# Seven-product pairs in a SwiGLU gate and up projection: four k-pairs of eight in place of three, with half of their weight sums added by DMA

## The chip, the cores and the metric

The kernel runs on one core of a Trainium2 chip. The metric is the time of one execution on the device in microseconds; lower is better. Three runs of the kernel before gave 2144.05 us in the median (2143.3 to 2145.18). The numbers are float32 throughout.

## The reference, cut to what matters

One decoder layer on 256 tokens of width 2048: a half feed-forward block, a mixing stage with three branches, and a second half feed-forward block of the same form. The change lies in the two feed-forward blocks:

```python
def swiglu_half_ffn(x, norm_g, w_gate_up, w_down):
    h = rmsnorm(x, norm_g)
    gate, up = jnp.split(h @ w_gate_up, 2, axis=-1)
    return 0.5 * ((jax.nn.silu(gate) * up) @ w_down)
```

`w_gate_up` is 2048 x 11264, its first 5632 columns for the gate and the others for up. `w_down` is 5632 x 2048.

## The kernel before, in words

**Two rounds for each product.** TensorE multiplies in `float32r`, a rounded float32. To keep float32 accuracy, each operand is cut in two: `cut` (L235) has ScalarE write the rounded value of a weight tile (`wh`), and VectorE write the rest, tile minus rounded tile (`wl`). The activations are cut in the same way when they are transposed. `add_product` (L240) then issues three matmuls of 128 x 128 by 128 x 512: high by high, low by high, high by low.

**Groups of the gate and up weights.** A feed-forward block (`ffn`, L412) handles the 5632 columns in eleven chunks of 512. Chunk 0 goes through `mm_group` (L320), the plain way. Each of the chunks 1 to 10 is one call of `pair_group` (L247, called at L467), so there are ten such groups in each block and twenty in the kernel. A group makes four 128 x 512 results in PSUM: two halves of the tokens (t) by gate and up (n). It goes through the 2048 rows of the weights in eight k-pairs of 2 x 128 rows. For each pair two DMAs of 512 KB on SP's queue (L268) bring the gate and the up part, 1 MB together, into a `raw` buffer. There are three `raw` buffers (L266), shared with `mm_group`.

**Plain pairs and seven-product pairs.** A plain pair costs 2 x 2 x 2 products of three matmuls, 24 matmuls. Its weights are cut in two calls on 1024 columns (L275). A k-pair can also be seen as a 2 x 2 by 2 x 2 product of blocks and done with seven products in place of eight (Winograd's form of Strassen's method), 21 matmuls. Then the activations are combined beforehand into a `form` page (`form_page`, L214), one for each such pair, and sums of the weight blocks are needed:

- L286: cut of the first two blocks `s0`, `s1` (`plain`)
- L288: `ta` = two sums, `s3+s1` and `s3+s2`, in one VectorE operation on 128 x 1024; L290: its cut (`hah`, `hal`)
- L292: cut of `s2` (`plain2`)
- L293, L294: `tb` = two more sums, `ta0+s2` and then that plus `s0`, each one VectorE operation on 128 x 512; L296: its cut (`hbh`, `hbl`)

The seven products read, in order, `plain` twice, `ha` twice, `plain2` once and `hb` twice (L299 to L307). After the last seven-product pair, L312 to L316 combine four extra PSUM banks (`p1`, `p5`, `p6`, `p7`) into terms that are added to the four results at the end. All eight banks come from one pool of eight; the transposes of the hidden activations take banks from it as well.

**Order.** The tuple `MIXED` (L24) lists the k-pairs in the order in which they are taken; the pairs with a number below the count of `form` pages are seven-product pairs. With three pages `MIXED` gives: plain 3, seven 0, plain 4, seven 1, plain 5, seven 2, plain 6, plain 7. Other steps (turning the hidden activations of the chunk before, and storing them) wait in a queue of side steps. `tick` runs one of them after each half of a plain pair that stands behind the last seven-product pair (L280), so four in a group. `drain` (L477) runs what is left before the down projection. The program is laid out by a planner that simulates the time of the program and sets, engine by engine, a fixed order from it; on the chip each engine works through its own list in order and waits at semaphores.

**Pools.** `wh` and `wl` have five buffers each of 1024 columns (L229). Pages of 4 KB a partition (30, L64) hold the activations, forms, `ta`, `tb`, `hah`, `hal`, `hbh` and `hbl`.

Of the kernel before, what the change touches and what calls it, by code (L numbers as in the profile page):

```python
# [9 lines left out]
F32 = mybir.dt.float32  # L10
# [10 lines left out]
KD = D // P  # L21
FF = 5632
NFC = FF // 512
MIXED = (3, 0, 4, 1, 5, 2, 6, 7)  # L24
KF = FF // P
EPS = 1e-6
# [6 lines left out]
def hybrid_layer(  # L33
# [210 lines left out]
                ps, sides[part], wt[i][:, col : col + 512], start=start and q == 0, stop=stop and q == 2  # L244
            )

    def pair_group(w, c0, c1, lhs, forms, order):  # L247

        seven = [u for u in order if u < len(forms)]
        acc = {}
        sums = {}
        terms = []
        kinds = [(0, 0), (1, 0), (0, 1), (1, 1)]

        def into(key, last):
            if key not in acc:
                acc[key] = bank("mm")  # L260
                return acc[key], True, last
            return acc[key], False, last

        for i, u in enumerate(order):
            end = i == len(order) - 1
            raw = wp.tile([P, 2, 2, 512], F32, tag="raw", name="raw")  # L266
            for n, cc in enumerate((c0, c1)):
                nc.sync.dma_start(  # L268
                    out=raw[:, n, :, :],
                    in_=w[2 * u * P : (2 * u + 2) * P, cc : cc + 512].rearrange("(k p) c -> p k c", p=P),  # L270
                )
            if u not in seven:
                for n in range(2):
                    wt = parts(1024)
                    cut(wt, raw[:, n, :, :].rearrange("p k c -> p (k c)"))  # L275
                    for t in range(T):
                        for kk in range(2):
                            ps, start, stop = into((t, n), end and kk == 1)
                            add_product(ps, [lhs(2 * u + kk, q, t) for q in range(2)], wt, kk * 512, start, stop)
                    if i > order.index(seven[-1]) if seven else True:  # L280
                        tick()
                continue
            last = u == seven[-1]
            s = raw.rearrange("p n k c -> p (n k) c")
            plain = parts(1024)
            cut(plain, s[:, 0:2, :].rearrange("p s c -> p (s c)"))  # L286
            ta, tb = page([2, 512], F32, "ta"), page([2, 512], F32, "tb")
            nc.vector.tensor_tensor(ta, s[:, 3:4, :].to_broadcast([P, 2, 512]), s[:, 1:3, :], ALU.add)  # L288
            ha = (page([1024], F32R, "hah"), page([1024], F32R, "hal"))
            cut(ha, ta.rearrange("p s c -> p (s c)"))  # L290
            plain2 = parts(512)
            cut(plain2, s[:, 2, :])  # L292
            nc.vector.tensor_tensor(tb[:, 0, :], ta[:, 0, :], s[:, 2, :], ALU.add)  # L293
            nc.vector.tensor_tensor(tb[:, 1, :], tb[:, 0, :], s[:, 0, :], ALU.add)  # L294
            hb = (page([1024], F32R, "hbh"), page([1024], F32R, "hbl"))
            cut(hb, tb.rearrange("p s c -> p (s c)"))  # L296
            fm = lambda m: [forms[u][:, q, m, :] for q in range(2)]
            xq = lambda kk, t: [lhs(2 * u + kk, q, t) for q in range(2)]
            for key, sides, wt, col in (  # L299
                ("p1", xq(1, 0), plain, 512),  # L300
                ((0, 0), xq(0, 0), plain, 0),
                ("p5", fm(0), ha, 0),
                ("p7", fm(2), ha, 512),
                ((0, 1), fm(3), plain2, 0),
                ("p6", fm(1), hb, 0),
                ((1, 0), xq(0, 1), hb, 512),
            ):  # L307
                ps, start, stop = into(key, last if isinstance(key, str) else end)
                add_product(ps, sides, wt, col, start, stop)
            if last:  # L310
                a, u3, u4, v = (temp([512], n) for n in ("ua", "u3", "u4", "uv"))
                nc.scalar.activation(a, acc["p1"], AF.Copy)  # L312
                nc.vector.tensor_tensor(u3, acc["p6"], a, ALU.add)
                nc.vector.tensor_tensor(u4, acc["p5"], u3, ALU.subtract)
                nc.vector.tensor_tensor(u3, acc["p7"], u3, ALU.add)
                nc.vector.tensor_tensor(v, acc["p5"], u3, ALU.subtract)  # L316
                terms = {(0, 0): a, (1, 0): u3, (0, 1): u4, (1, 1): v}
        return acc, terms
# [93 lines left out]
    def ffn(lx, forms, rs, wgu, wd, stream, cb, before=None):  # L412
        hid, flat = [], {}
        hdram = dp.tile([NFC - 1, P, 4 * S], F32, tag="hd", name="hd", bufs=2)
        rh = st.tile([P, T], F32, tag="rh", name="rh")

        def put(c, hd):

            dst = []

            def turn(jj):
                if jj == 0:
                    dst.append(page([4, S], F32, "hf"))
                ps = aux([2, S], "hid")
                for j in range(2):
                    for t in range(T):
                        k = 2 * jj + j
                        nc.tensor.transpose(ps[:, j, t * P : (t + 1) * P], hd[t][:, k * P : (k + 1) * P], ident)  # L428
                nc.scalar.activation(dst[0][:, 2 * jj : 2 * jj + 2, :], ps, AF.Copy)
                if jj == 1:  # L430
                    nc.sync.dma_start(out=hdram[c], in_=dst[0].rearrange("p k s -> p (k s)"))

            return [lambda: turn(0), lambda: turn(1)]

        def get(c):
            if c < NFC - 1:
                flat[c] = page([4, S], F32, "hg")
                nc.sync.dma_start(out=flat[c].rearrange("p k s -> p (k s)"), in_=hdram[c])

        def use(c):  # L440
            if c < NFC - 1:
                f = flat.pop(c)
                for jj in range(2):
                    hid.append(page([2, 2, S], F32R, "hid"))
                    split(hid[-1], 0, 2, f[:, 2 * jj : 2 * jj + 2, :])

        def gated(c, gate, up):
            hd = []
            for t in range(T):
                s = gate[t]  # L450
                if c == 0:
                    s = temp([512], "sg")
                nc.scalar.activation(s, gate[t], AF.Silu, scale=rs[0][:, t : t + 1])
                h = temp([512], "hd") if c == 0 else up[t]
                nc.vector.scalar_tensor_tensor(h, up[t], rh[:, t : t + 1], s, ALU.mult, ALU.mult)
                hd.append(h)
            return hd

        pa = mm_group(wgu, 0, KD, lx, before=before)
        nc.vector.tensor_scalar(rh, rs[0], 0.5, None, ALU.mult)  # L460
        pb = mm_group(wgu, FF, KD, lx)
        hd = gated(0, [pa[t][0] for t in range(T)], [pb[t][0] for t in range(T)])
        side.extend(put(0, hd))
        for c in range(1, NFC):
            if c == NFC - 1:
                side.extend(put_last)
            acc, terms = pair_group(wgu, c * 512, FF + c * 512, lx, forms, MIXED)  # L467
            for n in range(2):
                for t in range(T):
                    d = terms[t, n]  # L470
                    nc.vector.tensor_tensor(d, acc[t, n], d, ALU.add)
            hd = gated(c, [terms[t, 0] for t in range(T)], [terms[t, 1] for t in range(T)])
            if c < NFC - 1:
                side.extend(put(c, hd))
            if c == NFC - 2:
                put_last = [lambda: get(0), lambda: get(1)]
        drain()  # L477
        use(0)
        last = to_lhs(hid, lambda t: hd[t], None, "hid")

        def need(n, k0):
            if k0 == KF - 8:
                stream.load(n)
            if n > 0:
                return
            c = k0 // 4
            if c + 2 < NFC - 1:
                get(c + 2)
            if c + 1 < NFC - 1:
                use(c + 1)  # L490
            elif c + 1 == NFC - 1:
                for f in last:
                    f()

        lh = lhs_of(hid)
        for c in range(4):
            ps = mm_group(wd, c * 512, KF, lh, need=lambda k0, c=c: need(c, k0))
            cb(c, [[ps[t][0]] for t in range(T)])
# [29 lines left out]
        side.append(lambda c=c: prepare(c, 1))  # L528
    side.append(lambda: row_sums(range(4)) or rs0.append(row_rstd(ss0, "x0")))
    forms0 = []  # L530
    side.extend(form_steps(forms0, tiles0))
    side.append(small_loads)
    side.extend(pause * 3 + [small_cols])
    s0 = Stream([xv[:, :, c * 512 : (c + 1) * 512] for c in range(4)])
# [378 lines left out]
    side.extend(pause * 2)  # L913
    for n in range(2):
        cb(2 + n, sums(po, terms, n))
    side.extend(form_steps(forms2, x2))


    def store(c, ps):
# [37 lines left out]
```

## Time and profile before

| What | Value |
| --- | --- |
| Median of three runs | 2144.05 us (2143.3 to 2145.18) |
| The profiled execution's own time | 2142.92 us |
| Its span, first to last instruction | 2141.2 us, granted clock 1.00 |
| TensorE matmul busy | 2132.6 us |
| VectorE busy | 1572.0 us |
| ScalarE busy | 1135.9 us |
| GpSimd busy | 3.5 us |
| Read from HBM | 426.16 MB |

All three runs and the profiled execution lie within 2.3 us of each other. Busy time is the union of an engine's instructions. Matmuls are pipelined, and their ends are modelled, so the share of TensorE is no measure of its rate; the distance between the starts of matmuls is. `PEld` is the loading of the stationary operand. Idle time of an engine is put down to the engine or DMA that ended it. A row of the timeline gives start, duration, engine (`SPq` is the queue of DMA issues on SP), line, operation, what is written and what is read.

### The profile page before, as it was taken

To read this page: it belongs to the slowest core of one execution; us is meant where nothing else is said; L and a number is where in the kernel's file an instruction comes from. 1 tells how busy PE (TensorE), PEld (TensorE's weight loads), DVE (VectorE), ACT (ScalarE), POOL (GpSimd) and SP (SyncE) were. 2 spreads that over 40 slices of the span, in tenths; PEclk is the share of its full clock that TensorE was granted. 3 is DMA by queue.
4 is the path that set the end of the run, shared out by engine and by line. 5 is a ranking of instruction groups with operands and counts; after the bars stand their busy time and mean duration, and the time that the engine had idled before them with its cause. 6 is when DMAs were issued, how large, how long until landed. Compare 5 with 4: busy or idle time off the path is not lost.

```text
span 2141.2 us, 25671 instructions
## 1 busy us (share of the span) xinstructions
PE 2132.6 (100%) x9770; PEld 1761.2 (82%) x9770; DVE 1572.0 (73%) x1959; ACT 1135.9 (53%) x1412; POOL 3.5 (0%) x24
## 2 busy tenths in 40 slices
PE   9999999999999999999999999999999999999999
PEld 6888888888888888887788888888888888888887
DVE  7888899887454688657655778687899889974443
ACT  6555555555444565546644555555555555564332
POOL 0000000000000000000000000000000000000000
PEclk9999999999999999999999999999999999999999
DMA  7666666667666754754455656665666666686663
GB/s 256 206 210 215 208 207 222 208 237 280 201 215 206 236 177 156 246 171 144 141 194 196 198 185 217 224 219 197 207 216 208 213 209 208 220 309 227 206 206 108
DMA packets 219679, 444.63 MB, mean 208 GB/s; under 512 B 10830, under 2 KB 11940, under 8 KB 219556
## 3 DMA queue, kind: packets, MB, share of 16 engines
q1 hardware_dynamic: 219264, 442.95, 62.3%
q8 instruction: 76, 1.25, 0.2%
q14 instruction: 47, 0.39, 0.0%
q10 hardware_dynamic: 292, 0.05, 0.0%
HBM read 426.16 MB, written 16.79 MB: 207 GB/s over the span
## 4 chain that ended last, share of the span: by engine, by line
PE 99%; DMA 1%; ACT 0%; issue 0%; DVE 0%; SPq 0%; ACTq 0%
PE mm L350 48%; PE mm L243 47%; PE hid L428 1%; DMA raw<-in_ffn_w_gate_up_dram 1%; PE x L199 0%; PE fpt L835 0%; PE fav L845 0%; ACT junk L362 0%; PE mg L199 0%; PE memT L199 0%; PE flg L807 0%; PE mav L740 0%; PE mlg L713 0%; PE flg L805 0%; PE fav L847 0%; PE fav L846 0%
## 5 line engine op out<-in xcount | busy, mean ns | idle before, releaser
L344 DVE TENSOR_TENSOR wl<-raw,wh 128x1024 fp32r<-128x1024 f32 (+2 forms) x393 | 471.2, 1200 | 380.2 <-ACT wh L343 379.4
L343 ACT ACTIVATE wh<-raw 128x1024 fp32r<-128x1024 f32 (+2 forms) x393 | 407.9, 1040 | 495.5 <-PE mm L350 435.6
L243 PE MATMUL mm<-wh,x 128*128 128x512 f32 x2116 | 656.7, 391 | 0.0
L237 ACT ACTIVATE wh<-raw 128x1024 fp32r<-128x1024 f32 (+1 forms) x384 | 375.4, 980 | 382.5 <-PE mm L243 194.6
L238 DVE TENSOR_TENSOR wl<-raw,wh 128x1024 fp32r<-128x1024 f32 (+1 forms) x384 | 426.4, 1122 | 102.4 <-ACT wh L237 101.9
L243 PEld LDWEIGHTS mm<-wh,x 128*128 128x128 f32 x2116 | 394.2, 188 | 80.1
L350 PE MATMUL mm<-wh,hid 128*128 128x512 f32 x1408 | 435.6, 390 | 0.0
L243 PE MATMUL mm<-wl,x 128*128 128x512 f32 x1058 | 411.3, 390 | 0.0
L350 PE MATMUL mm<-wh,x 128*128 128x512 f32 (+1 forms) x1216 | 371.3, 383 | 2.9 <-ACT wh L343 1.6
L350 PEld LDWEIGHTS mm<-wh,hid 128*128 128x128 f32 x1408 | 264.3, 188 | 54.8
L350 PE MATMUL mm<-wl,hid 128*128 128x512 f32 x704 | 274.0, 389 | 0.0
L350 PEld LDWEIGHTS mm<-wh,x 128*128 128x128 f32 x1216 | 223.8, 188 | 48.4 <-issue 2.9
L243 PEld LDWEIGHTS mm<-wl,x 128*128 128x128 f32 x1058 | 198.6, 188 | 41.8
L350 PE MATMUL mm<-wl,x 128*128 128x512 f32 (+1 forms) x608 | 231.2, 381 | 0.5 <-DVE wl L344 0.5
L350 PEld LDWEIGHTS mm<-wl,hid 128*128 128x128 f32 x704 | 132.2, 188 | 27.2
L350 PEld LDWEIGHTS mm<-wl,x 128*128 128x128 f32 x608 | 114.3, 188 | 21.6 <-DVE wl L344 1.0
L288 DVE TENSOR_TENSOR ta<-raw 128x1024 f32<-128x1024 f32 x72 | 87.9, 1220 | 14.4 <-DMA raw<-in_w_out_dram 6.9
L237 ACT ACTIVATE hah<-ta 128x1024 fp32r<-128x1024 f32 x72 | 75.9, 1054 | 28.8 <-DVE ta L288 28.8
L238 DVE TENSOR_TENSOR hal<-ta,hah 128x1024 fp32r<-128x1024 f32 x72 | 88.0, 1222 | 4.2 <-ACT hah L237 4.2
L243 PE MATMUL mm<-hah,form 128*128 128x512 f32 x288 | 88.3, 389 | 0.0
L238 DVE TENSOR_TENSOR hbl<-tb,hbh 128x1024 fp32r<-128x1024 f32 x72 | 87.9, 1221 | 0.0
L237 ACT ACTIVATE hbh<-tb 128x1024 fp32r<-128x1024 f32 x72 | 75.8, 1052 | 16.5 <-DVE tb L294 16.5
(319 smaller groups left out, 1924.3 us busy)
## 6 DMA issues: line engine op xcount, KB each, us to landing
raw<-in_ffn_w_gate_up_dram SPq DMA_DIRECT2D x321, 512.0 KB, 4.6
raw<-in_ffn_w_down_dram SPq DMA_DIRECT2D x88, 1024.0 KB, 5.2
raw<-in_w_in_dram SPq DMA_DIRECT2D x52, 1024.0 KB, 5.2
raw<-in_w_in_dram SPq DMA_DIRECT2D x48, 512.0 KB, 4.1
raw<-in_ffn_w_gate_up_dram SPq DMA_DIRECT2D x15, 1024.0 KB, 6.9
hd<-hf SPq DMA_DIRECT2D x20, 512.0 KB, 5.2
hg<-hd SPq DMA_DIRECT2D x20, 512.0 KB, 6.9
raw<-in_w_mem_kv_dram SPq DMA_DIRECT2D x8, 1024.0 KB, 5.2
```

Of the source, the lines that this page charges most:

```text
L237: nc.scalar.activation(dst[0], src, AF.Copy)
L238: nc.vector.tensor_tensor(dst[1], src, dst[0].bitcast(F32), ALU.subtract)
L243: nc.tensor.matmul(ps, sides[part], wt[i][:, col : col + 512], start=start and q == 0, stop=stop and q == 2)
L288: nc.vector.tensor_tensor(ta, s[:, 3:4, :].to_broadcast([P, 2, 512]), s[:, 1:3, :], ALU.add)
L343: nc.scalar.activation(hv, rv, AF.Copy)
L344: nc.vector.tensor_tensor(lv, rv, hv.bitcast(F32), ALU.subtract)
L350: nc.tensor.matmul(ps[t][i][:, :n], lhs(k, part, t), wt[:, kk, o : o + n], start=k == 0 and q == 0, stop=k == kt - 1 and q == 2,)
L428: nc.tensor.transpose(ps[:, j, t * P : (t + 1) * P], hd[t][:, k * P : (k + 1) * P], ident)
```

## The change

Three edits. The gate and up groups take their k-pairs in a new order, `HALF`, and both feed-forward blocks prepare four `form` pages in place of three, so that pairs 0 to 3 are seven-product pairs and pairs 4 to 7 are plain. The other callers of `pair_group` keep `MIXED` and three pages. In the gate and up groups alone (`by_dma=True`), `tb` is no tile of its own: the two further sums are added in place to `ta`, after `ta` has been cut, by three DMAs on GpSimd's queue that add their source to their destination, 256 KB each: `ta1 += s1`, `ta0 += s2`, `ta1 += s0`. The third writes the half that the first wrote. With `s3+s2` in `ta1` beforehand, the results are the same two sums as `tb` held.

```diff
+HALF = (4, 0, 5, 1, 6, 2, 3, 7)
 MIXED = (3, 0, 4, 1, 5, 2, 6, 7)
...
-    def pair_group(w, c0, c1, lhs, forms, order):
+    def pair_group(w, c0, c1, lhs, forms, order, by_dma=False):
...
-            ta, tb = page([2, 512], F32, "ta"), page([2, 512], F32, "tb")
+            ta = page([2, 512], F32, "ta")
+            tb = ta if by_dma else page([2, 512], F32, "tb")
             nc.vector.tensor_tensor(ta, s[:, 3:4, :].to_broadcast([P, 2, 512]), s[:, 1:3, :], ALU.add)
             ha = (page([1024], F32R, "hah"), page([1024], F32R, "hal"))
             cut(ha, ta.rearrange("p s c -> p (s c)"))
             plain2 = parts(512)
             cut(plain2, s[:, 2, :])
-            nc.vector.tensor_tensor(tb[:, 0, :], ta[:, 0, :], s[:, 2, :], ALU.add)
-            nc.vector.tensor_tensor(tb[:, 1, :], tb[:, 0, :], s[:, 0, :], ALU.add)
+            if by_dma:
+                for at_, one in ((1, 1), (0, 2), (1, 0)):
+                    nc.gpsimd.dma_start(out=ta[:, at_, :], in_=s[:, one, :], accum_op=ALU.add)
+            else:
+                nc.vector.tensor_tensor(tb[:, 0, :], ta[:, 0, :], s[:, 2, :], ALU.add)
+                nc.vector.tensor_tensor(tb[:, 1, :], tb[:, 0, :], s[:, 0, :], ALU.add)
...
-            acc, terms = pair_group(wgu, c * 512, FF + c * 512, lx, forms, MIXED)
+            acc, terms = pair_group(wgu, c * 512, FF + c * 512, lx, forms, HALF, by_dma=True)
...
-    side.extend(form_steps(forms0, tiles0))
+    side.extend(form_steps(forms0, tiles0, 4))
...
-    side.extend(form_steps(forms2, x2))
+    side.extend(form_steps(forms2, x2, 4))
```

## The prediction

> **What bounds the kernel now.** I read the page's busy times first, then the chain that ended last, then the stretches of one group.
>
> ```profile
> PE 2132.6 (100%) x9770; PEld 1761.2 (82%) x9770; DVE 1572.0 (73%) x1959; ACT 1135.9 (53%) x1412; POOL 3.5 (0%) x24
> PE 99%; DMA 1%; ACT 0%; issue 0%; DVE 0%; SPq 0%; ACTq 0%
> ...
> 180.12 38.79 PE mm L243 x171
> 222.57 38.79 PE mm L243 x171
> ...
> core 0: us, PE busy (x) PEld busy (x) DVE busy (x) ACT busy (x) POOL busy (x), PEclk, DMA share, GB/s
> 10.00:33.00 23.00, 20.60 (x100) 16.10 (x99) 18.22 (x38) 18.26 (x37) 0.00 (x0) 1.00 0.96 341
> 180.12:222.57 42.45, 42.45 (x193) 35.14 (x192) 37.50 (x42) 24.23 (x28) 0.00 (x0) 1.00 0.64 211
> ```
>
> TensorE carries 99% of the chain. In a gate and up group it steps from matmul to matmul every 38.79/171 = 0.2268 us without a hole, and a group takes 42.45 us. VectorE follows at 37.5 of 42.45, ScalarE at 24.2; the DMA engines are 64% busy. So a matmul less is 0.227 us less, as long as weights arrive in time. How that supply works is the question.
>
> ```profile
> SPq L268 <- DVE wl L238: 589.2, 135, 7.3
> SPq L268 <- DVE tb L294: 139.4, 38, 10.1
> ...
> 184.63 0.88 SPq L268 DMA_DIRECT2D raw<-in_ffn_w_gate_up_dram  x2
> 191.69 0.88 SPq L268 DMA_DIRECT2D raw<-in_ffn_w_gate_up_dram  x2
> 195.81 0.88 SPq L268 DMA_DIRECT2D raw<-in_ffn_w_gate_up_dram  x2
> 200.78 0.88 SPq L268 DMA_DIRECT2D raw<-in_ffn_w_gate_up_dram  x2
> 204.99 0.88 SPq L268 DMA_DIRECT2D raw<-in_ffn_w_gate_up_dram  x2
> ...
> 198.40 1.23 DVE L288 TENSOR_TENSOR ta<-raw 128x1024 f32<-128x1024 f32 x1 [0.30 <-DMA raw<-in_ffn_w_gate_up_dram]
> 199.54 1.22 DVE L238 TENSOR_TENSOR wl<-raw,wh 128x1024 fp32r<-128x1024 f32 x1
> 200.75 1.23 DVE L238 TENSOR_TENSOR hal<-ta,hah 128x1024 fp32r<-128x1024 f32 x1
> 204.23 0.69 DVE L294 TENSOR_TENSOR tb<-tb,raw 128x512 f32<-128x512 f32 x1
> 211.27 0.62 PE L243 MATMUL mm<-wh,x 128*128 128x512 f32 x2
> ```
>
> SP's queue always waits for a `raw` buffer to come free: the last reader is the cut (L238) or the second `tb` add (L294). The ring of three is full all the time. A seven-product pair's load goes out at 191.69, VectorE finds it landed at 198.40 (L = 6.7 us), `hal` ends at 201.98 (3.6 us later), the last `tb` add at 204.92, and the next load leaves at 204.99: 13.3 us in the buffer. The plain pair loaded at 184.63 keeps its buffer until the cut that ends at 200.76: 16.1 us, partly waiting for TensorE to give back `wh`. TensorE first uses the pair of 198.40 at 211.27; with its first cut done by 200.76 the lead is 10.5 us.
>
> **The change part by part.** TensorE: now 5 x 24 + 3 x 21 = 183 matmuls a group, then 4 x 24 + 4 x 21 = 180. Three fewer are 0.68 us, in twenty groups 13.6 us; a group could take 41.77 us. All of it is on the path today.
>
> ```profile
> L237 ACT ACTIVATE wh<-raw 128x1024 fp32r<-128x1024 f32 x312 | 330.2, 1060 | 338.3 <-PE mm L243 182.4 <-DVE u L315 53.5 <-issue 49.6
> L238 DVE TENSOR_TENSOR wl<-raw,wh 128x1024 fp32r<-128x1024 f32 x312 | 381.1, 1222 | 102.4 <-ACT wh L237 101.9
> L288 DVE TENSOR_TENSOR ta<-raw 128x1024 f32<-128x1024 f32 x72 | 87.9, 1220 | 14.4 <-DMA raw<-in_w_out_dram 6.9 <-DMA raw<-in_ffn_w_gate_up_dram 6.2 <-DMA raw<-in_w_in_dram 1.0
> L238 DVE TENSOR_TENSOR hal<-ta,hah 128x1024 fp32r<-128x1024 f32 x72 | 88.0, 1222 | 4.2 <-ACT hah L237 4.2
> L237 ACT ACTIVATE hah<-ta 128x1024 fp32r<-128x1024 f32 x72 | 75.9, 1054 | 28.8 <-DVE ta L288 28.8
> L294 DVE TENSOR_TENSOR tb<-tb,raw 128x512 f32<-128x512 f32 x72 | 49.4, 686 | 0.0
> L293 DVE TENSOR_TENSOR tb<-ta,raw 128x512 f32<-128x512 f32 x72 | 49.4, 686 | 0.0
> L238 DVE TENSOR_TENSOR wl<-raw,wh 128x512 fp32r<-128x512 f32 x72 | 49.4, 686 | 0.0
> L237 ACT ACTIVATE wh<-raw 128x512 fp32r<-128x512 f32 x72 | 45.4, 631 | 44.2 <-issue 29.8 <-PE mm L243 12.2 <-PE mm L350 1.1
> L313 DVE TENSOR_TENSOR u<-mm,ua 128x512 f32<-128x512 f32 x24 | 16.6, 692 | 11.7 <-PE mm L243 11.7
> ```
>
> VectorE: six adds leave a group (6 x 0.686 = 4.1 us), and one plain pair (2 x 1.22) becomes a pair of four long operations and a short one (4 x 1.22 + 0.69), which adds 3.1. That gives 36.5 of 41.77 us; with all eight adds it would be 42.0, too much. ScalarE gains 3 x 1.06 + 0.63 - 2.12 = 1.7 and stands at 25.9. Both fit as sums. The fourth form page is seven more short operations in each block, under 0.7 us each (as L313), beside `mm_group`; nothing there waits for it.
>
> Side steps: behind the last seven-product pair stands one plain pair, so two ticks are left for the two turning steps; in the first block the longer queue lags by a step and `drain` takes the rest. I cost this at nothing: the stored activations are fetched again only after the last group, and SP's list allows that early. Uncovered it would be one landing in each block, 6.9 us (`hg` below). The four extra banks must be free one plain pair (24 x 0.227 = 5.4 us) after the last seven-product pair; their four VectorE operations take 2.8 us. Nothing again.
>
> The accumulating DMAs: twelve a group, 256 KB each, three in each of four pairs. No row shows one.
>
> ```profile
> DMA  6999469930028992798058956895017992799100
> ...
> q1 hardware_dynamic: 4496, 8.91, 63.2%
> ...
> raw<-in_ffn_w_gate_up_dram SPq DMA_DIRECT2D x321, 512.0 KB, 4.6
> hd<-hf SPq DMA_DIRECT2D x20, 512.0 KB, 5.2
> hg<-hd SPq DMA_DIRECT2D x20, 512.0 KB, 6.9
> ...
> rows<-in_ffn_norm_dram ACTq DMA_DIRECT2D x2, 8.0 KB, 3.8
> ```
>
> *Engine time.* The first two rows are of the stretch 180.12 to 222.57: a packet of 2 KB holds an engine 0.632 x 42.45 x 16 / 4496 = 95 ns. A row of the tile is 2 KB, so a DMA is 128/16 = 8 packets on each engine: 0.76 us if an accumulate costs one pass, 1.53 if reading source and destination costs two. Below one pass it cannot be, since every byte is written. A group's DMA work goes from 27.2 us (0.64) to 36.3 or 45.5 us, shares of 0.87 or 1.09 of 41.77. The highest share that a stretch shows is 0.96. At two passes the DMA engines alone would hold a group at 45.5/0.96 = 47.4 us. The row of digits shows that they work in bursts with holes, so even one pass delays loads in flight. I add 1.2 us to each load: 1.5 accumulates a pair are 1.1 to 2.3 us. The Trainium skill (Collectives: The Full Stack, section The bandwidth ceiling: the fold count and why AG ≠ RS ≠ AR) says that an add in the DMA path needs two source reads on one ring and measured half the rate of a copy; no row here shows an add. By that rule two passes would be right, and the group would stand at 47.4 us or above.
>
> *Latency.* The third DMA writes where the first wrote, so two follow each other, after both cuts of `ta`. From issue to landing the trace has 3.8 us (8 KB) at the short end and 6.9 (`hg`) at the long one; I take 5.2, the store out of SBUF, as an accumulate's source lies there too. The chain C is then 10.4 us (7.6 to 13.8), where the two adds took 2.9. Queued behind it: on ScalarE the cut `hbh` and all cuts listed behind it, on VectorE `hbl`, on GpSimd the next pair's DMAs, on TensorE the products p6 and (1,0), and on SP the next load, since the third DMA is now the last reader of `raw`.
>
> *The ring.* A seven-product pair holds a buffer for 6.7 + 1.2 + 3.6 + 10.4 = 21.9 us. A plain pair needs at least 6.7 + 1.06 + 2 x 1.22 = 10.2 and took 16.1 above; I take the middle, 13.2, plus 1.2 = 14.4. Four of each through three buffers: 4 x 36.3 / 3 = 48.4 us a group, 5.9 more than now. Twenty groups cost 118 us. The lead of 10.5 us is used up first, once in each block: minus 21. The sum is 2142.9 + 97 = 2240 us. The profiled execution (2142.92, with a span of 2141.2) is 1.1 below the median of 2144.05, less than any term here.
>
> **The rivals.** *The accumulates land early.* Three buffers feed 41.77 us a group if one pair of each kind holds them for 31.3 us together; with 14.4 for the plain one and 11.5 ahead of the chain, C must be at most 5.4 us, 2.7 each. If plain pairs shrink to their least (11.4), 8.4 us will do, 4.2 each. Then TensorE keeps the bound and all its gain: 2142.9 - 13.6 = 2129 us. For it: TensorE's lead, plain pairs that wait without need, and the 3.8 us row. Against: landings of 4.6 and more for loads of this size and larger, with the engines fuller than now. The Trainium skill (DMA: Bandwidth & Descriptors, section Anatomy of one DMA — SWDGE (gpsimd) path) fits about 2.0 us plus bytes at 436 GB/s, which would be 2.6 us for 256 KB, an estimate from that page; by it this rival wins, though the trace's loads take longer than that fit.
>
> *The DMA engines bound.* If an accumulate costs three passes (two reads and a write one after the other, 2.3 us), a group is (27.2 + 27.5)/0.96 = 57 us, and the sum 2142.9 + 20 x 14.5 - 21 = 2412 us. No row speaks for or against.
>
> *It cancels.* A group at 42.4 us, no change: C of about 6 us with plain pairs at their middle.
>
> *It doesn't do what it says*, if the fourth page comes too late for a block's first group: the first block has 17 ticks before it and the page is the thirteenth step, so I give it nothing.
>
> **How the numbers follow.** A measurement of this kernel can tell about 0.2% (4.3 us) from no change. The ring-bound case has 0.60, DMA-bound or a longer chain 0.15, early landing 0.20, no change 0.05. So faster 0.20, same 0.05, slower 0.75. The forecast is the ring's 2240. Its own range goes from 2160 (C at its short end, plain pairs at 14.4: 44.6 us a group, 2143 + 43 - 21, about 2165, less a little) to 2340 (C at 13.8: 52.9 us, 2143 + 209 - 21 = 2331, and a little for ScalarE's order). The whole range takes in the early case as well: 2128 to 2340.
>
> **What would show it.** Right: groups of 46 to 52 us; TensorE waits in them for `hbh` or `wh`; SP's loads (L268) wait for accumulating DMAs and for nothing else so long; a load's buffer kept over 20 us in seven-product pairs; landings of the accumulates near 5 us; a DMA share of 0.75 to 0.95. Wrong: groups of 41.8 us with 180 matmuls in one unbroken row, or accumulates that land within 3 us. A DMA share at 0.96 throughout would speak for the second rival.

## The result, and the profile after

The changed kernel takes 2611.49 us in the median of four runs (2608.6 to 2612.85); the kernel before took 2144.39 us beside it. The ratio is 1.2176, with a 95% interval of 1.2157 to 1.2195. The forecast was 2240 us, at most 2340: the sign came out as forecast, the size did not. 467 us were added where 97 were expected.

The page of the changed kernel, its busy times, its DMA queues, its chain of waits and its DMA issues:

```profile
PE 2244.3 (86%) x9710; PEld 1802.3 (69%) x9710; DVE 1566.0 (60%) x1911; ACT 1161.6 (44%) x1454; POOL 209.5 (8%) x264
...
q0 software_dynamic: 34560, 62.93, 14.7%
...
PE 56%; DMA 20%; issue 9%; DVE 6%; POOL 4%; ACT 4%; SPq 0%; POOLq 0%; ACTq 0%; DVEq 0%
...
raw<-in_ffn_w_gate_up_dram SPq DMA_DIRECT2D x321, 512.0 KB, 4.8
...
ta<-raw POOLq DMA_DIRECT2D x240, 256.0 KB, 4.3
```

No engine is the bound any more. TensorE's part of the chain fell from 99% to 56%; the rest is spread over DMA, VectorE, ScalarE, GpSimd and issue. A chain that goes through every engine and through the DMA queues, while all of them have idle time, is the mark of steps that follow each other. Two gate and up groups by stretches (TensorE, its loads, VectorE, ScalarE, GpSimd busy; granted clock; DMA share; GB/s):

```profile
108.50:175.90 67.40, 48.95 (x188) 37.80 (x188) 36.96 (x38) 25.84 (x30) 10.29 (x12) 0.83 0.67 179
242.49:309.50 67.01, 49.19 (x189) 37.82 (x189) 37.03 (x39) 25.41 (x30) 10.29 (x12) 0.81 0.67 180
```

A group takes 67 us in place of 42.45. VectorE and ScalarE do the work that the prediction gave them (37.0 and 25.4 for 36.5 and 25.9). The DMA engines are busy for 0.67 x 67.0 = 44.9 us, and 45.5 was the figure for two passes. So the amounts of work were right, and the group is longer than any of them. The waits of the same kernel (in total, times, longest):

```profile
ACT wh L238 <- DMA raw<-in_ffn_w_gate_up_dram: 344.5, 110, 7.4
PEld mm L244 <- ACT hbh L238: 335.5, 57, 11.5
PE mm L244 <- ACT hbh L238: 308.7, 55, 11.1
...
ACT hbh L238 <- DMA ta<-raw: 291.0, 74, 10.5
DVE hbl L239 <- ACT hbh L238: 257.4, 61, 9.9
...
SPq L269 <- DMA ta<-raw: 750.6, 112, 13.1
```

TensorE waits for `hbh`, `hbh` for the accumulating DMAs, and SP's loads (L269) for the same DMAs. This is what the prediction named. What it did not see stands in the timeline. These are rows of one stretch of the changed kernel, of VectorE, GpSimd, SP's loads, ScalarE and TensorE one after the other:

```profile
208.97 1.23 DVE L239 TENSOR_TENSOR hbl<-ta,hbh 128x1024 fp32r<-128x1024 f32 x1 [2.69 <-ACT hbh L238]
210.11 1.22 DVE L290 TENSOR_TENSOR ta<-raw 128x1024 f32<-128x1024 f32 x1
...
222.62 1.22 DVE L239 TENSOR_TENSOR wl<-raw,wh 128x1024 fp32r<-128x1024 f32 x1 [5.95 <-ACT wh L238]
...
227.69 1.23 DVE L239 TENSOR_TENSOR hbl<-ta,hbh 128x1024 fp32r<-128x1024 f32 x1
228.84 1.22 DVE L290 TENSOR_TENSOR ta<-raw 128x1024 f32<-128x1024 f32 x1
231.47 1.23 DVE L239 TENSOR_TENSOR wl<-raw,wh 128x1024 fp32r<-128x1024 f32 x1 [1.41 <-ACT wh L238]
232.61 1.22 DVE L239 TENSOR_TENSOR hal<-ta,hah 128x1024 fp32r<-128x1024 f32 x1
...
242.47 1.23 DVE L239 TENSOR_TENSOR hbl<-ta,hbh 128x1024 fp32r<-128x1024 f32 x1 [8.04 <-ACT hbh L238]
243.61 1.22 DVE L290 TENSOR_TENSOR ta<-raw 128x1024 f32<-128x1024 f32 x1
...
234.35 1.72 POOL L297 DMA_DIRECT2D ta<-raw  x2 [12.74 <-DVE hal L239]
237.99 0.85 POOL L297 DMA_DIRECT2D ta<-raw  x1 [1.91 <-DMA ta<-raw]
...
226.60 2.06 SPq L269 DMA_DIRECT2D raw<-in_ffn_w_gate_up_dram  x4
...
241.37 0.88 SPq L269 DMA_DIRECT2D raw<-in_ffn_w_gate_up_dram  x2
...
230.38 1.06 ACT L238 ACTIVATE wh<-raw 128x1024 fp32r<-128x1024 f32 x1 [2.71 <-DMA raw<-in_ffn_w_gate_up_dram]
...
241.38 1.06 ACT L238 ACTIVATE hbh<-ta 128x1024 fp32r<-128x1024 f32 x1 [8.48 <-DMA ta<-raw]
...
217.85 0.62 PE L244 MATMUL mm<-wh,x 128*128 128x512 f32 x2
218.31 0.61 PE L244 MATMUL mm<-wl,x 128*128 128x512 f32 x2
...
227.72 1.22 PE L244 MATMUL mm<-hbh,form 128*128 128x512 f32 x2 [7.67 <-ACT hbh L238]
228.74 1.05 PE L244 MATMUL mm<-hbh,x 128*128 128x512 f32 x2
229.59 0.63 PE L244 MATMUL mm<-hbl,form 128*128 128x512 f32 x1
...
242.49 0.80 PE L244 MATMUL mm<-hbh,form 128*128 128x512 f32 x1 [7.13 <-ACT hbh L238]
...
244.36 1.05 PE L244 MATMUL mm<-wh,x 128*128 128x512 f32 x2
```

Read VectorE's rows first. Each `ta` stands right behind the `hbl` of the pair before it: 208.97 and 210.11, 227.69 and 228.84, 242.47 and 243.61. So the next pair's first sum starts only when the pair before has its accumulates landed and its second cut made. Its own load is not what it waits for: the `ta` of 243.61 reads a load that left with the four of 226.60 at the latest, since the next one leaves at 241.37, and no load of this stretch landed in under 3.3 us. Follow one pair: `ta` 228.84, `hal` 232.61, two DMAs 234.35, the third 237.99, `hbh` 241.38, `hbl` 242.47, and only then the next `ta` at 243.61, 14.8 us later. GpSimd's two DMAs had waited 12.74 us for `hal`: GpSimd is idle between chains, not late. Four such chains, one after the other, make the group: 67.0 / 4 = 16.75 us each (14.7 to 19.2).

The ring of `raw` buffers lies in this chain too. Between `ta` and `hal` of the pair followed, `wl` (231.47) stands first in VectorE's list; it needs `wh` (230.38), which waited for a load that left at 226.60, when the accumulates of the pair before had landed and given back their buffer.

TensorE's list adds to it. TensorE stands still for 7.67 us before 227.72 and for 7.13 before 242.49, because the products with `hbh` come next. Products of other weights, cut from 222.62 on, were ready meanwhile; in the list they stand behind, and start at 244.36.

### The profile page after: what moved, and what is told of

It reads as the page before. It is cut to its first block, busy times and chain, and to the rows that moved or that the text cites. A ratio compares the mean times of both kernels' runs of the same rounds, so it can differ in the third digit from the quotient of the medians.

```text
span 2611.1 us, 26275 instructions
## 1 busy us (share of the span) xinstructions
PE 2244.3 (86%) x9710; PEld 1802.3 (69%) x9710; DVE 1566.0 (60%) x1911; ACT 1161.6 (44%) x1454; POOL 209.5 (8%) x264
## 3 DMA queue, kind: packets, MB, share of 16 engines
q0 software_dynamic: 34560, 62.93, 14.7%
## 4 chain that ended last, share of the span: by engine, by line
PE 56%; DMA 20%; issue 9%; DVE 6%; POOL 4%; ACT 4%; SPq 0%; POOLq 0%; ACTq 0%; DVEq 0%
PE mm L356 39%; PE mm L244 15%; DMA ta<-raw 12%; DMA raw<-in_ffn_w_gate_up_dram 7%; POOL ta L297 4%; DVE hal L239 3%; ACT wh L238 2%; DVE wl L239 2%; ACT hbh L238 1%; ACT hah L238 1%; DVE ta L290 1%; DMA hg<-hd 1%; SPq L269 0%; PE hid L434 0%; PE x L200 0%
## 5 line engine op out<-in xcount | busy, mean ns | idle before, releaser
L244 PE MATMUL mm<-wh,x 128*128 128x512 f32 x1876 | 588.6, 400 | 7.7 <-ACT wh L238 7.7
L238 ACT ACTIVATE wh<-raw 128x1024 fp32r<-128x1024 f32 (+1 forms) x384 | 362.1, 952 | 506.7 <-DMA raw<-in_ffn_w_gate_up_dram 344.5
L244 PEld LDWEIGHTS mm<-wh,x 128*128 128x128 f32 x1876 | 362.7, 194 | 91.9 <-ACT wh L238 14.6
L244 PE MATMUL mm<-wl,x 128*128 128x512 f32 x938 | 359.3, 398 | 0.6
L244 PE MATMUL mm<-hbh,form 128*128 128x512 f32 x184 | 82.8, 540 | 308.8 <-ACT hbh L238 308.7
L297 POOL DMA_DIRECT2D ta<-raw x240 | 206.0, 960 | 1663.1 <-DVE hal L239 1089.5
L244 PEld LDWEIGHTS mm<-hbh,form 128*128 128x128 f32 x184 | 38.2, 241 | 338.2 <-ACT hbh L238 335.5
L356 PEld LDWEIGHTS mm<-wh,x 128*128 128x128 f32 x1216 | 223.9, 188 | 48.9 <-issue 2.9
L239 DVE TENSOR_TENSOR hbl<-ta,hbh 128x1024 fp32r<-128x1024 f32 x80 | 98.0, 1225 | 257.6 <-ACT hbh L238 257.4
L238 ACT ACTIVATE hbh<-ta 128x1024 fp32r<-128x1024 f32 x80 | 84.6, 1058 | 291.4 <-DMA ta<-raw 291.0
L244 PEld LDWEIGHTS mm<-wl,x 128*128 128x128 f32 x938 | 180.8, 193 | 41.4 <-DVE wl L239 2.9
L244 PE MATMUL mm<-hah,form 128*128 128x512 f32 x368 | 119.0, 434 | 36.0 <-ACT hah L238 35.8
L356 PEld LDWEIGHTS mm<-wl,x 128*128 128x128 f32 x608 | 114.3, 188 | 21.4 <-DVE wl L350 1.0
```

Of the source, the lines that this page charges most:

```text
L238: nc.scalar.activation(dst[0], src, AF.Copy)
L239: nc.vector.tensor_tensor(dst[1], src, dst[0].bitcast(F32), ALU.subtract)
L244: nc.tensor.matmul(ps, sides[part], wt[i][:, col : col + 512], start=start and q == 0, stop=stop and q == 2)
L297: nc.gpsimd.dma_start(out=ta[:, at_, :], in_=s[:, one, :], accum_op=ALU.add)
L356: nc.tensor.matmul(ps[t][i][:, :n], lhs(k, part, t), wt[:, kk, o : o + n], start=k == 0 and q == 0, stop=k == kt - 1 and q == 2,)
```

## The experiments

What 20 groups cost over the kernel before is turned into a mean group by (time - 2143) / 20 + 42.45; for the changed kernel that gives 65.9 us, beside the 67.0 of the two groups above. A time given without an interval is that of one execution. Each edit is made to the changed kernel unless said otherwise, and the lines in a kernel's rows are its own. The suspects are: the serial chain (the order of the lists), the ring of `raw` buffers, the DMA engines' time, and the new k-pair order with its fourth page.

**All sums on VectorE, the new order kept.**

```diff
-            acc, terms = pair_group(wgu, c * 512, FF + c * 512, lx, forms, HALF, by_dma=True)
+            acc, terms = pair_group(wgu, c * 512, FF + c * 512, lx, forms, HALF)
```

> The DMA part undone: four seven-product pairs in the order HALF, the sums tb again two adds on VectorE. Both theories put the loss on the accumulating DMAs, so the 467 us are gone. Left is VectorE: by the sum of the prediction 42.0 us of work for a group of 41.77, though neighbouring operations overlap at their ends by about 0.1 us, so nearer 40.5. Expected 2130 to 2150 us, a group of 41.8 to 42.5 us; over 2200 would mean that the order HALF itself, with two seven-product pairs next to each other, costs.

Measured: 2210.18 us, ratio 1.0311 (1.0297 to 1.0325). The expectation missed. So 66 of the 467 us come without any DMA, and 401 with the DMAs. Waits of this kernel:

```profile
ACT hbh L238 <- DVE tb L300: 95.1, 52, 3.3
...
PEld mm L244 <- ACT hbh L238: 38.0, 15, 4.3
...
PE mm L244 <- ACT hbh L238: 32.0, 15, 3.8
```

TensorE waits for `hbh` here too, with no landing in the chain.

**The old order with three pages, the sums by DMA.**

```diff
-            acc, terms = pair_group(wgu, c * 512, FF + c * 512, lx, forms, HALF, by_dma=True)
+            acc, terms = pair_group(wgu, c * 512, FF + c * 512, lx, forms, MIXED, by_dma=True)
...
-    side.extend(form_steps(forms0, tiles0, 4))
+    side.extend(form_steps(forms0, tiles0))
...
-    side.extend(form_steps(forms2, x2, 4))
+    side.extend(form_steps(forms2, x2))
```

> The DMA part alone: three seven-product pairs in the old order MIXED, tb made by the three accumulating DMAs. Serial theory: the next pair's ta stands behind the hbl of the pair before in VectorE's list, so chains (ta, hah, hal, two accumulates one after the other, hbh, hbl, 67/4 = 16.7 us each in the changed kernel) do not overlap; three of them are 50 us a group, 2143 + 20 x 7.8 = about 2300 us. Ring theory (three raw buffers, 21.9 us for a seven-product pair and 14.4 for a plain one): (3 x 21.9 + 5 x 14.4)/3 = 45.9 us a group, about 2190 us.

Measured: 2353.38 us, a group of 53 us. That is above both figures, 53 us from the serial one and 163 from the ring's. Three chains of 16.75 are 50 us; the accumulates landed after 5.1 us here, where 4.3 lie in the 16.75. The cost goes with the count of chains.

**One landing in place of two in series.** The third accumulate is an add on VectorE; the other two run side by side.

```diff
-                for at_, one in ((1, 1), (0, 2), (1, 0)):
+                for at_, one in ((1, 1), (0, 2)):
                     nc.gpsimd.dma_start(out=ta[:, at_, :], in_=s[:, one, :], accum_op=ALU.add)
+                nc.vector.tensor_tensor(ta[:, 1, :], ta[:, 1, :], s[:, 0, :], ALU.add)
```

> The changed kernel with the third accumulate replaced by a VectorE add into the same half, so two DMAs run side by side and the chain has one landing in place of two. Serial theory: a chain of 16.7 us loses about 5.5 us (one landing with its issue) and gains 0.7 us, 11.9 x 4 = 48 us a group, about 2250 us. Ring theory: the buffer time of a seven-product pair falls by 4.5 us only on the ring, from the measured 67 us a group by 4 x 4.5/3 = 6 us, 61 us, about 2500 us.

Measured: 2453.97 us, 58 us a group, 14.5 a chain: between the two expectations. The second landing is worth 158 us, and one landing in the chain still costs 244 over the sums on VectorE. A chain became 2 us shorter, less than half a landing; what took up the rest was not followed.

**Plain copies in place of the accumulates.** This kernel leaves out the further sums and so computes something else; every DMA and every wait stays.

```diff
-                    nc.gpsimd.dma_start(out=ta[:, at_, :], in_=s[:, one, :], accum_op=ALU.add)
+                    nc.gpsimd.dma_start(out=ta[:, at_, :], in_=s[:, one, :])
```

> The changed kernel with its twelve DMAs a group as plain copies in place of accumulates, so the two sums are left out and the output is another one. All waits stay. An accumulate held an engine for about 200 ns a row of 2 KB, twice a copy's 95; a copy should take 95 to 105 ns, each landing 0.8 us less, two of them in each of four chains: 6.4 us a group less at most, 2480 to 2540 us. If the adding itself were what costs, it would come near 2240 us.

Measured: 2468.67 us. Queue and landing of this kernel, to be set beside those of the changed kernel above:

```profile
q0 software_dynamic: 19200, 62.93, 6.9%
...
ta<-raw POOLq DMA_DIRECT2D x240, 256.0 KB, 2.6
```

A copy of 256 KB takes 0.069 x 2466.9 / 240 = 0.71 us of each of the 16 engines, an accumulate 0.147 x 2611.1 / 240 = 1.60 us. It lands after 2.6 us, an accumulate after 4.3. Two landings shorter by 1.7 us in 80 chains would be 272 us at most; the copies save 143.

**A fourth `raw` buffer.** (In both places where `raw` is made; 28 common pages, to make room.)

```diff
-            raw = wp.tile([P, 2, 2, 512], F32, tag="raw", name="raw")
+            raw = wp.tile([P, 2, 2, 512], F32, tag="raw", name="raw", bufs=4)
```

> The changed kernel with four raw buffers in place of three (and 28 pages in place of 30, to make room). Ring theory: a group falls to about three quarters, 67 x 3/4 = 50 us, about 2290 us. Serial theory: the chains still stand one behind the other, the group stays above 62 us, 2550 to 2620 us.

Measured: 2593.07 us, 18 less. The ring alone isn't the cause, and with that my own theory of the prediction fell. The ring did go out of the chain: the waits of `wh` for loads fell from 344.5 us in total to 53.4. But those of `hbh` for the accumulates rose from 291.0 to 480.1, so the order of the lists holds the chains one behind the other without it.

**Own pages for `hbh` and `hbl`.** This changes neither the work nor the DMAs, only which buffers the second cut is written to, and with it the order that the planner can set.

```diff
-    pp = ctx.enter_context(tc.tile_pool(name="pg", bufs=30))
+    pp = ctx.enter_context(tc.tile_pool(name="pg", bufs=26))
...
-            hb = (page([1024], F32R, "hbh"), page([1024], F32R, "hbl"))
+            hb = tuple(pp.tile([P, 1024], F32R, tag="hb", name=n, bufs=4) for n in ("hbh", "hbl"))
```

> The changed kernel with the four pages hbh and hbl taken from a pool of their own (four buffers, the common pool cut from 30 to 26). In all kernels run so far ta of the next pair stands right behind hbl of the pair before. Theory: pages of one pool are handed out in the order of the program, so ta, hah and hal of the next pair, which come after hbh and hbl in the program, cannot be listed before them, and each chain (two landings) keeps the next one waiting. With a pool of their own chains overlap and the ring of three raw buffers is left: 45 to 52 us a group, 2200 to 2340 us. Rival: the planner lists hbl first because it takes a landing to be short; then the pool changes nothing, 2550 to 2620 us.

Measured: 2357.09 us, 254 less, 53 us a group. VectorE's timeline of this kernel:

```profile
258.82 1.23 DVE L290 TENSOR_TENSOR ta<-raw 128x1024 f32<-128x1024 f32 x1 [1.20 <-DMA raw<-in_ffn_w_gate_up_dram]
...
261.17 1.23 DVE L239 TENSOR_TENSOR hal<-ta,hah 128x1024 fp32r<-128x1024 f32 x1 [0.52 <-ACT hah L238]
266.00 1.23 DVE L239 TENSOR_TENSOR hbl<-ta,hbh 128x1024 fp32r<-128x1024 f32 x1 [3.61 <-ACT hbh L238]
...
271.94 1.23 DVE L290 TENSOR_TENSOR ta<-raw 128x1024 f32<-128x1024 f32 x1 [1.81 <-DMA raw<-in_ffn_w_gate_up_dram]
```

`ta` and `hal` at 258.82 and 261.17 now stand ahead of the `hbl` at 266.00, which belongs to the pair before. `ta` waits for its load instead of for a chain.

**One pool again, but the second cut and its products written later in the program**, behind the next pair's `ta`, `ha` and DMAs. Pages and buffers are those of the changed kernel.

```diff
...
+            def rest(tb=tb, u=u, products=products, six=fm(1), ten=xq(0, 1)):
+                hb = (page([1024], F32R, "hbh"), page([1024], F32R, "hbl"))
+                cut(hb, tb.rearrange("p s c -> p (s c)"))
+                products((("p6", six, hb, 0), ((1, 0), ten, hb, 512)))
...
+            while late:
+                late.pop()()
...
+            late.append(rest)
+            if last:
+                late.pop()()
```

> The changed kernel with one pool as it is, but the cut of hbh and hbl and the two products that read them stand in the program behind the next pair's ta, hah, hal and its DMAs (the last seven-product pair of a group keeps its place). Theory of the pool order: the next pair's ta no longer waits, as with the pool of its own, 2200 to 2400 us; somewhat above that run, since the last pair of each group still holds the next group's first one back. Rival (price of a landing in the planner): no change, above 2550 us.

Measured: 2327.38 us, 284 less, 51.7 us a group. VectorE's timeline of this kernel:

```profile
260.05 1.22 DVE L291 TENSOR_TENSOR ta<-raw 128x1024 f32<-128x1024 f32 x1
...
267.07 1.22 DVE L291 TENSOR_TENSOR ta<-raw 128x1024 f32<-128x1024 f32 x1
...
274.66 1.23 DVE L239 TENSOR_TENSOR hbl<-ta,hbh 128x1024 fp32r<-128x1024 f32 x1
```

The second pair's `ta` (267.07) stands ahead of the first pair's `hbl` (274.66). Two edits that share nothing but the order of the lists give back 254 and 284 us. That order is the main cause. It changed on ScalarE and TensorE as well, so the share of VectorE's list alone is not shown.

**The later second cut with four `raw` buffers, and the same with copies.** The later second cut and the fourth buffer together; then `accum_op` left out as well, and with it again the sums.

> The version with the cut of hbh and hbl late in the program (2327 us, 51.6 us a group), and four raw buffers in place of three (28 common pages in place of 30). With the order of the pages out of the way the ring of raw buffers should be what is left: 51.6 x 3/4 = 38.7 us, so the ring no longer binds, and the DMA engines do: 27.2 us of loads and 12 x 1.6 us of accumulates are 46.4 us a group, less where loads run back to back: 43 to 48 us, 2150 to 2260 us. Rival: what is left is the planned order on ScalarE and VectorE, which takes a landing to be shorter than it is; then the fourth buffer brings little, above 2290 us.

> The version with late hb and four raw buffers (2279 us, DMA share 0.89 to 0.93 in its groups) with the twelve DMAs as plain copies: the sums are left out and the output is another one, every wait stays. A copy of 256 KB takes 0.71 us of the 16 engines, an accumulate 1.60. If the DMA engines' time holds that version, a group loses about 10 us of DMA work (27 + 8.5 = 36 us) and falls to TensorE's or VectorE's bound, 42 to 44 us, 2140 to 2180 us. If the order of the lists with two landings one behind the other holds it, two landings of 2.6 in place of 5.6 us give back part, 2200 to 2250 us.

Measured: 2278.98 us with accumulates (49.2 us a group), 2163.56 with copies. Stretches of the second feed-forward block, the first row of the accumulating kernel, the second row of the copying one:

```profile
1700.00:2030.00 330.00, 291.97 (x1261) 233.00 (x1259) 246.56 (x259) 168.71 (x197) 67.18 (x78) 0.98 0.93 254
```

```profile
1700.00:2000.00 300.00, 295.94 (x1315) 242.57 (x1314) 237.11 (x253) 171.22 (x199) 32.12 (x60) 0.99 0.81 285
```

With the chain overlapped and buffers to spare, the DMA engines are busy for 0.93 of the time, and the accumulates land after 5.6 us. With copies the share is 0.81, and TensorE is nearly gapless. The 115 us between them are what accumulating costs over copying, by engine time or by the later landing (5.6 us to 4.2). 2163.56 lies in the range expected if engine time holds the first kernel, but both fell together, and the two can't be separated here.

**The same with all sums on VectorE.** (The later second cut, four `raw` buffers, `by_dma` left out.)

> No DMA part: four seven-product pairs with all adds on VectorE, the cut of hbh and hbl late in the program, four raw buffers, 28 common pages. With the pool of its own and three raw buffers this version took 2142.8 us, with waits for raw loads in the first block. If the ring was what kept it from the 13.6 us of TensorE time, it gains now: 2130 to 2138 us. If VectorE is full, 2138 to 2150 us.

Measured: 2158.27 us, ratio 1.0073 (1.006 to 1.0087), where less was expected. On this base the copies cost 5 us and the accumulates 121, beside the sums on VectorE.

**One landing, with the chain overlapped.** First with own pages, then with the later second cut and four buffers.

> One landing in place of two (two accumulates side by side, the third sum on VectorE) with the pages hbh and hbl from a pool of their own. By the ring of the prediction with the measured landing of 4.4 us: 6.7 + 1.2 + 3.6 + 5 + 0.7 = 17.2 us for a seven-product pair and 14.4 for a plain one, 42.1 us a group: 2130 to 2190 us. DMA work is 27.2 + 8 x 1.6 = 40 us of 41.8, VectorE 39.2. If a landing grows under that load to 6 us, 44 us a group, 2180 us.

> Two accumulates side by side and one VectorE add in all four pairs, the cut of hbh and hbl late in the program, four raw buffers, 28 pages. Neither ring nor order of the pages should bind; DMA work 40 us and VectorE 39.2 us of 41.8. 2130 to 2170 us; if it stays above the version of the same call with three buffers, the order planned on the engines is what holds it.

Measured: 2211.47 us (1.0318, 1.0301 to 1.0335) and 2185.38 us (1.0196, 1.0181 to 1.0211). Both missed, on the slow side.

**Two accumulates in each of two pairs only.** Own pages; pairs 1 and 3 as in the kernels with one landing, pairs 0 and 2 on VectorE.

> Four seven-product pairs, pages hbh and hbl from a pool of their own; in pairs 1 and 3 two accumulates side by side and one VectorE add, in pairs 0 and 2 all adds on VectorE. VectorE 36.5 + 6 x 0.69 = 40.6 us of a group of 41.8 (by durations; by starts about 38), DMA work 27.2 + 4 x 1.6 = 33.6 us, one chain in every other seven-product pair. If the version with all adds on VectorE was held by VectorE, this one gains on it: 2130 to 2142 us. If the landing still holds up the lists of ScalarE and VectorE, 2150 to 2200 us.

Measured: 2178.49 us, ratio 1.0158 (1.0143 to 1.0173). Even four accumulates a group in place of twelve cost more than VectorE's adds.

**No DMA, own pages**, and as a control the kernel before with own pages.

> Four seven-product pairs with all adds on VectorE (as in the run that undid the DMA part), hbh and hbl from a pool of their own. Theory of the pool order: the 67 us that this version lost to the kernel before come from the same order of ta behind hbl, with two seven-product pairs next to each other; most of it returns, 2135 to 2165 us, and if VectorE has room, 2130. Rival: VectorE is simply full (42.0 us of work in a group of 41.8); then 2195 to 2215 us as without the pool.

> The kernel before, with hbh and hbl from a pool of their own and nothing else: a control for the fastest version. TensorE carried 99% of its chain already, so the pool alone should bring nothing, 2142 to 2145 us; then the gain of the fastest version is that of the fourth seven-product pair, which the pool and the mended side steps let through. Below 2139 us the pool itself would have a part in it.

Measured: 2142.82 us, ratio 0.9997 (0.9988 to 1.0006), for the first and 2143.97 us, ratio 1.0001 (0.9992 to 1.001), for the control. Own pages take all 67 us off the first experiment and do nothing for the kernel before. Four seven-product pairs cost nothing now, but they bring nothing either.

**What hides the gain: other places for the pairs, and one empty side step less.** In the first block the fourth page is one more step ahead of the others; `pause` is an empty step.

```diff
-HALF = (4, 0, 5, 1, 6, 2, 3, 7)
+HALF = (0, 4, 1, 5, 2, 6, 3, 7)
```

```diff
-    side.extend(pause * 3 + [small_cols])
+    side.extend(pause * 2 + [small_cols])
```

> All adds on VectorE, hbh and hbl from a pool of their own, and the order 0, 4, 1, 5, 2, 6, 3, 7, in which no two seven-product pairs stand next to each other within a group. If the pair of neighbours (2, 3) is what VectorE cannot keep up with, 2131 to 2140 us; if VectorE is full over the whole group, 2142 to 2150 us; slower if the four extra banks, needed at the very start of a group, are not free yet, up to 2180 us.

> All adds on VectorE, hbh and hbl from a pool of their own, three raw buffers, and one empty side step fewer in the first block, so that the fourth form page no longer makes the queue of side steps lag by one in the first block's groups. The first block's groups are then laid out as the second's. If the lag cost: 2134 to 2141 us; if not, 2142 to 2144 us.

Measured, each on the kernel of own pages without DMA: 2170.71 us (1.0126, 1.0113 to 1.014) for the other places, a loss whose cause was not followed; 2135.26 us (2133.84 to 2135.78) with the empty step gone, ratio 0.996 (0.9947 to 0.9972). This is the fastest version, 8.4 us below the 2143.7 of the kernel before beside it. The chain of the kernel with three empty steps:

```profile
PE 91%; DVE 6%; DMA 1%; issue 1%; ACT 0%; SPq 0%; DVEq 0%; ACTq 0%
```

The chain, and one stretch of the first block, with two:

```profile
PE 98%; DVE 1%; DMA 0%; ACT 0%; SPq 0%; issue 0%; ACTq 0%; DVEq 0%
...
60.00:440.00 380.00, 379.89 (x1706) 313.14 (x1706) 362.94 (x406) 229.22 (x260) 0.00 (x0) 1.00 0.61 211
```

VectorE left the chain and TensorE is gapless, although VectorE is busy for 362.94 of 380 us. Why the lists around the lagging steps were worse was not followed further.

## Why the prediction was wrong, by its steps

**The step that failed is the ring:** "A seven-product pair holds a buffer for 6.7 + 1.2 + 3.6 + 10.4 = 21.9 us", four of each kind through three buffers, 48.4 us a group. It lets each pair's chain begin when its load has landed, whatever the pair before is doing. In the changed kernel the chains don't overlap. A group is four of them in a row, 16.75 us each, 67 us. The kernel did come out slower, as forecast, and the waits named were there; but the step that costs most is in no term of the sum. More buffers changed little (2593); putting the second cut elsewhere in the order changed much (2357 and 2327). This was to be seen ahead. VectorE's list in the kernel before:

```profile
196.87 1.23 DVE L238 TENSOR_TENSOR hbl<-tb,hbh 128x1024 fp32r<-128x1024 f32 x1
198.40 1.23 DVE L288 TENSOR_TENSOR ta<-raw 128x1024 f32<-128x1024 f32 x1 [0.30 <-DMA raw<-in_ffn_w_gate_up_dram]
```

There too `ta` follows `hbl`. It cost nothing while three short chains fitted into 42 us: own pages gain nothing there (2143.97). The prediction did list what is queued behind the chain on each engine, "on VectorE `hbl`", but not what stands behind `hbl`. That the common pages set this order because they are handed out as the program asks for them (`hbh` and `hbl` of one pair ahead of `ta` of the next) is inferred: pages of their own change the order, and how the planner comes to it was not looked at. That the order makes the time is shown.

**Once the chains overlap, the ring's figure is near:** 51.7 to 53.2 us a group against 48.4 and a range up to 52.9. There landings are 4.9 to 5.5 us, where 5.2 was taken. That the ring sets these groups is shown in part only: a fourth buffer takes 2.4 us off the 51.7, and the DMA engines are busy for 0.85 to 0.88 of the time.

**TensorE's lead was read too long.** The prediction uses the cut that ends at 200.76 twice, as the plain pair's last one and as the first one of the pair of 198.40. The second reading is wrong. The load of 200.78 takes the buffer that this cut gives back, so the cut is the plain pair's. The other pair's first cut is the first of the two in this row of the kernel before, done at about 203.7:

```profile
202.49 1.82 DVE L238 TENSOR_TENSOR wl<-raw,wh 128x1024 fp32r<-128x1024 f32 x2
```

The lead is about 7.6 us and not 10.5, which adds 6 us to the sum, little beside the miss.

**Engine time:** 1.60 us measured, near the 1.53 of two passes (one pass, 0.76, was left open), where a copy cost 0.71. The Trainium skill (Collectives: The Full Stack, section The bandwidth ceiling: the fold count and why AG ≠ RS ≠ AR) says of the rings of collectives that an add needs two source reads on one ring, and so runs at half the rate of a copy. The trace agrees in kind: 2.3 times the time of a copy. The second rival took three passes and 57 us a group, and these are not what the runs show. The prediction's floor for two passes, 47.4 us at a share of 0.96, comes near what is left with the serial order and the ring gone, 49.2 us at 0.93; whether the engines' time or the landings hold that kernel stays open.

**Landing:** 4.3 us in the changed kernel, shorter than the 5.2 taken, and longer than the 2.7 that early landing needed. In the pair followed above 7.0 us pass from the first two DMAs to `hbh`, where C was taken at 10.4. So the chain was not underpriced here; it was counted as overlapping. The Trainium skill's fit for GpSimd's DMAs (DMA: Bandwidth & Descriptors, section Anatomy of one DMA — SWDGE (gpsimd) path) gives 2.6 us for this size, an estimate from that page. The copies took that in the first kernel with copies and 4.2 us in the second, whose DMA engines are fuller (0.81 against 0.61 from 1700 to 2000); the accumulates took 4.3 to 5.6 us in all kernels.

**VectorE:** 36.5 forecast, 37.0 measured. That all eight adds would be "too much" at 42.0 of 41.77 was wrong: the fastest version has them all there, with VectorE busy for 362.94 of 380 us. **Side steps at nothing** was wrong as well: with own pages and no DMAs, one empty step decides over 7.6 us. **TensorE's gain** of 13.6 us shows as 8.4 at best.

**The 467 us, then:** 254 to 284 are the serial order. From 2327 a fourth buffer takes 48, and copies for accumulates another 115; at 2164, 20 us above the kernel before, 5 are left for DMAs of any kind, since the same kernel with VectorE's sums takes 2158. The other 15 are there without DMAs too, and their cause stays open. These parts belong to this order of the edits: the fourth buffer was worth 48 us here and 18 by itself.

**What would show it:** TensorE waiting for `hbh`, SP's loads for the accumulates, landings near 5 us: these came (4.3 for the last). Groups of 46 to 52 us did not (67), nor did the DMA share (0.67 for 0.75 to 0.95). A share below forecast beside a group longer than forecast says that the cost is a chain, not an amount.

**Not tried:** the accumulates with own pages and four `raw` buffers together, and the changed kernel with one empty step less and nothing else.

## What to carry to other kernels

When a slow step is put between two operations, walk each engine's list past the operation that waits: what stands behind it, and is that the start of the next round? If so, rounds that overlapped on paper run one behind the other, and the cost is their sum. Moving adds from an engine with idle time to accumulating DMAs pays in latency and in DMA time at once; here four such pairs beat both kernels with the adds left on VectorE, own pages for the second cut and one empty step less.

## What the runs showed of the hardware

An accumulating DMA inside SBUF held the engines 2.3 times as long as a copy of the same 256 KB (1.60 to 0.71 us) and landed 1.7 us later (4.3 to 2.6). Landings were longer in the kernels whose DMA engines were busier: 5.6 us for the accumulates at a share of 0.93, and 4.2 for the copies at 0.81.

TensorE paid for a hole twice here. In the timeline of the changed kernel two matmuls take 0.46 us before the hole (217.85 to 218.31) and 0.85 behind it (228.74 to 229.59), and the granted clock of such a group is 0.81. A group's 189 matmuls, the transposes among them, are busy for 49.2 us; in the kernel before, 193 take 42.45. The Trainium skill (TensorE: Matmul & The Clock Gate, Part 1: The HAM clock gate) says that an idle window of about 3.4 us drops the array to half its rate. The holes of 7 to 8 us agree with that.
